# A two-layer hybrid backbone on one core: first output tile issued around the last attention unit's close, key copies ordered for the maxima, output tile steps with raised priority, wider lags

## The chip, the cores and the metric

The kernel runs on one core of one Trainium2 chip. The metric is device microseconds (us) from start to end of one execution. A core has TensorE (PE in the rows; PEld is its weight load), VectorE (DVE), ScalarE (ACT), GpSimd (POOL) and SyncE (SP). In this kernel SP issues nearly all transfers, in its program's order.

## The reference

Two layers work on 1024 latent tokens and 256 context tokens of 1024 features. Shortened to what matters:

```python
for l in range(DEPTH):                                    # DEPTH = 2
    mod_x = silu(c) @ w_ada[l] + b_ada[l]                 # shift, scale, gate
    hx, hc = modulate(x, ...), modulate(ctx, ...)         # RMS norm, scale, shift
    u_x, u_c = hx @ w_in[l], hc @ w_in[l]                 # one projection, cut into the branches
    a_x = rmsnorm(gdn_bidir(q, k, v, g, beta)) * silu(z)  # gated delta rule, chunks of 64, two directions
    b_x = softmax_attention(q_x, cat(k_x, k_c), cat(v_x, v_c)) * silu(z_b)    # 4 heads
    c_x = b_gate * dwconv(c_gate * h) * silu(z_c)
    x = x + gate_x * (cat(a_x, b_x, c_x) @ w_out[l])
    ...                                                   # the same for ctx in layer 0
return rmsnorm(x, final_norm_g)
```

The delta rule needs, for each 128 tokens, direction and head, the inverse of a triangular matrix.

## The kernel before

The tokens are ten tiles of 128 (tiles 8 and 9 are the context), in three groups: 512, 512 and 256 tokens. Matmuls that need float32 precision are three: operands are split into a high and a low part (`split`, L75 on ACT for the high part, L76 on DVE or POOL for the low one), and `mm3` (L84) and the blocks (L452) add hi·hi, lo·hi and hi·lo.

The order of the program is written by a planner. Pieces of work are generators ("lanes"), each `yield x` of which asks to be resumed when x us of planned matmul work have gone by; between them the main line emits block matmuls and calls `sch.tick`. What comes out is one program order. A scheduler then orders each engine's instructions by priority, with `tc.high_priority` to raise some. TensorE keeps the written order from the delta recurrence on (`in_order`) until the last attention unit's close. Tiles live in small pools that are used round: "P2" has 7 buffers for the raw weight slices `wr`, the gates `zb`, `ot` and `za` of the output tiles, the rows `mk` and `mq` of the attention projections and others, so that a load there waits for the reader of the buffer's previous tile.

In a layer these stages matter here:

- The **modulation** lane (`Ada`): 512 KB slices `wa` are loaded (L184), and the next resumption multiplies them (L188). In layer 0 the last of these run beside the projection.
- The **projection**: `run_blocks` multiplies weight blocks with all groups (L452), 24 matmuls for 512 tokens and 24 of half width for 256. Beside it the triangular inverses are made: `base_inverse` (L680, L681, DVE) and `merge`, one lane for each of the ten tiles, which joins 32-blocks to 64 and 128: four small matmul steps (L720, L729/L732, L746, L755) with copies on ACT and DVE between them, and a store of the result `nn_d` (L760).
- **Keys and values**: `kv_lane`, one for each tile, waits until merges are done, loads `mk` (L824), transposes it (L827, L828) and copies it (ACT, L79) to `ckv` and `pes`. From `pes` the position rows go by DMA into the key tensors `kh`, `kl` and `kc` (L1058, high, low and context). `q_rows` (L854, L855) does the like for queries.
- **Attention** in units of a token group and two heads. `a_max` (L1102, L1104) takes row maxima over the keys, `a_shift` (L1113, L1117) turns them and sends them into the queries, `a_scores` (L84, L1143) and `a_pv` (L1159) are the scores, exponentials and values; the exponentials are summed tile by tile on POOL (L1129), and the closing adds of the last key step of a unit's first head, and of both heads in the last unit, on DVE (L1127). `a_out` (L1166 to L1176) closes a unit: sums by matmul (L1170), reciprocal, gate. The first unit's maxima stand in a prologue with `k_pair` (keys of two heads) and `v_tile` (values of a tile).
- The **output**: `load_wo` brings the 16 slices of `w_out` (L1327) and splits them into two halves of 512 columns, `wo[0]` and `wo[1]`. `finish(i)`, one for each output tile, loads `ot`, `raw` and `za`, scales `ot` by its root mean square (squares L1344 on ACT, L1345 to L1349 on DVE and POOL), transposes it (L1353), multiplies by the gate (L1354), splits the result into `mix`, and multiplies it with both halves: 24 matmuls of 512 columns each (L84).

Of the kernel before, what the change touches and what calls it, by code (L numbers as in the profile page):

```python
# [18 lines left out]
EPS = 1e-6  # L19
# [9 lines left out]
def kernel(  # L29
# [27 lines left out]
    def st(shape, tag, dtype=F32, name=None):  # L57
        return sb.tile(shape, dtype, tag=tag, name=name or tag, bufs=BUFS[tag])
# [19 lines left out]
    def copy_a(out, in_):  # L78
        A.activation(out=out, in_=in_, func=ACTF.Copy)  # L79
# [97 lines left out]
    class Ada:  # L177
# [42 lines left out]
        def lane(self):  # L220
            todo = [(t, q, k4) for t in self.thirds for q in range(4) for k4 in range(2)]

            def get(n):
                wa = st([128, 4, 256], "P4", name="wa")
                self.load(*todo[n], wa)
                return wa

            for n, (t, q, k4) in enumerate(todo):
                if k4 == 0:
                    brow = self.bias(q) if t == 2 else None  # L230
                    pm = bank()
                wa = get(n)
                yield 6.5
                self.mm(k4, wa, pm)
                if k4 == 1:
                    yield 1.5
                    yield from self.close(t, q, pm, brow)
# [78 lines left out]
    for l in range(DEPTH):  # L316
# [372 lines left out]
        def merge(i, bt, tl):  # L689
            while not based.ok(bt):  # L690
                yield 1.0
            M = st([128, 4, 128], "P2", name="Mm")
            S.dma_start(out=M, in_=mm_d[i])
# [13 lines left out]
            with tc.high_priority(offset=400):  # L707
# [3 lines left out]
                for bk in range(4):  # L711
                    r = slice(32 * bk, 32 * bk + 32)
                    co = 32 * (bk % 2)
                    copy_a(nt6[r, :, co:co + 32], ntr[r, bk // 2])
            yield
            prs = ((0, 0, 1), (1, 1, 0), (0, 2, 3), (1, 3, 2))
# [5 lines left out]
            with tc.high_priority(offset=400):  # L722
                A.activation(out=Z, in_=z3, func=ACTF.Copy, scale=-1.0)
            yield
            n3 = bank()[:, 0:128].rearrange("p (h c) -> p h c", h=4)
# [8 lines left out]
            with tc.high_priority(offset=400):  # L734
# [4 lines left out]
                for q, (d, a, e) in enumerate(prs):  # L739
                    copy_a(N[32 * a:32 * a + 32, d, :, 32 * e:32 * e + 32], n3[32 * a:32 * a + 32])  # L740
            yield
            z23 = bank()[:, 0:256].rearrange("p (h c) -> p h c", h=4)
# [97 lines left out]
        def q_rows(g):  # L840
# [7 lines left out]
            if g < 2:  # L848
                rot = st([128, 512], "P2", name="rot")
                S.dma_start(out=rot[64:128], in_=rot_in[:, t0:t0 + n])  # L850
            yield 3.0
            pt0, pt1 = bank(), bank()
# [208 lines left out]
        def k_pair(h0):  # L1061
            ws = wk[:, :, 64 * h0:64 * h0 + 128]
            for g in (0, 1, 2):
                t0, n = GROUPS[g]
                cs = slice(t0, t0 + n)
                pk = bank()
                mm3(pk[:, 0:n], ((ws[:, 0], ckv[0][:, cs]), (ws[:, 0], ckv[1][:, cs]), (ws[:, 1], ckv[0][:, cs])))
                for r in range(2):
                    h = h0 + r
                    hi, lo = (kh[:, h, cs], kl[:, h, cs]) if g < 2 else (kc[:, 0, h, :], kc[:, 1, h, :])  # L1070
                    pr = pk[64 * r:64 * r + 64, 0:n]
                    copy_a(hi[0:64], pr)
                    if r:
                        kr = st([128, 512], "P2", name="kr")[0:64, 0:n]
                        copy_a(kr, pr)
                        P.tensor_tensor(lo[0:64], kr, hi[0:64].bitcast(F32), ALU.subtract)
                    else:
                        V.tensor_tensor(out=lo[0:64], in0=pr, in1=hi[0:64].bitcast(F32), op=ALU.subtract)
                yield


# [37 lines left out]
        def a_sums(u, kts, pts, rs=(0, 1)):  # L1119
            n = GROUPS[u["g"]][1]  # L1120
            keys = a_keys(u["g"])
            for r in rs:
                acc = vt[:, 5 + r, 0:n]
                ab_ = [pts[r][:, kk, 0:n] for kk in range(2)]
                for a0, a1 in [(ab_[0], ab_[1])] if kts[0] == keys[0] else [(acc, ab_[0]), (acc, ab_[1])]:
                    if kts[-1] == keys[-1] and (r == 0 or u is units[-1]):
                        V.tensor_tensor(out=acc, in0=a0, in1=a1, op=ALU.add)  # L1127
                    else:
                        P.tensor_tensor(acc, a0, a1, ALU.add)  # L1129
# [168 lines left out]
        v_tile(7)  # L1298
        a_shift(units[0])
        v_tile(8)  # L1300
        v_tile(9)
        for _ in k2:
            pass
        sch.tick(1.0)
        nu = len(units)
# [18 lines left out]
        def load_wo_half(q, wh, wl):  # L1324
            for k in range(KD):
                wr = st([128, 512], "P2", name="wr")
                S.dma_start(out=wr, in_=w_out[l, 128 * k:128 * k + 128, 512 * q:512 * q + 512])  # L1327
                yield 1.5
                split(wr, wh[:, k], wl[:, k], P if k % 2 else V)
                yield 1.5  # L1330

        def finish(i):
# [9 lines left out]
            jk = st([128, 128], "h5", name="jk4")  # L1342
            for h in range(4):
                A.activation(out=jk, in_=ot[:, h], func=ACTF.Square, accum_out=so[:, h:h + 1])  # L1344
            V.scalar_tensor_tensor(out=so, in0=so, scalar=1.0 / 128, in1=s_2[:, :, i], op0=ALU.mult, op1=ALU.mult)  # L1345
            P.tensor_scalar(so, so, 1.0, EPS, ALU.mult, ALU.add)
            P.tensor_tensor(so, so, nhalf[:, 0:4], ALU.pow)
            V.tensor_tensor(out=so, in0=so, in1=s_1[:, :, i], op=ALU.mult)
            V.tensor_tensor(out=ot, in0=ot, in1=bc(so, 128), op=ALU.mult)  # L1349
# [4 lines left out]
            V.scalar_tensor_tensor(out=raw[:, 0:4, :], in0=pt.rearrange("p (h f) -> p h f", h=4), scalar=col[:, 74:75], in1=za,  # L1354
                                   op0=ALU.mult, op1=ALU.mult)
            mix = st([128, 2, KD, 128], "W8", F32R, name="mix")
            split(raw[:, 0:4], mix[:, 0, 0:4], mix[:, 1, 0:4])
            split(raw[:, 4:8], mix[:, 0, 4:8], mix[:, 1, 4:8], P)
            xt = load_x(l, i)
            done[i] = xt  # L1360
            yield 3.5
            for q in range(2):
# [7 lines left out]
                if last:  # L1370
                    if q == 0:
                        sf = st([128, 2], "st", name="sf")
                    A.activation(out=tm, in_=xt[:, cs], func=ACTF.Square, scale=D ** -0.5, accum_out=sf[:, q:q + 1])
            if not last:
                S.dma_start(out=xs_d[i], in_=xt)
                return
# [29 lines left out]
        for x_, u in enumerate(units):  # L1406
# [12 lines left out]
            for q, kts in enumerate(steps):  # L1419
# [129 lines left out]
```

## Time and profile before

| | us |
|---|---|
| runs of the kernel | 1716.41, 1718.66, 1720.2 |
| their median | 1718.66 |
| the profiled execution, start to end | 1723.55 |
| its span, first to last instruction | 1721.8 |
| TensorE busy in the span | 1650.5 |

The granted clock is TensorE's share of full speed as the profile records it: 0.978 in the mean. Layer 0 takes about the first 950 us, layer 1 the rest. TensorE is busy nearly all the time, so that its idle stretches and what follows them are what to read; a table of waits gives, for each place, the total, how often, and the longest.

### The profile page before, as it was taken

What the parts mean: (1) busy time and instruction counts of PE and PEld (TensorE: products, weight loads), DVE (VectorE), ACT (ScalarE), POOL (GpSimd) and SP (SyncE); (2) the same over time, 40 slices, a digit from 0 to 9 for tenths busy, and PEclk for the clock granted to TensorE, in tenths of its full rate; (3) what the DMA queues carried; (4) which work ended last, traced back from release to release, by engine and by line L of the source; (5) the groups of instructions that cost most, each with busy time, mean ns of one, the idle gap of its engine ahead of it and who ended that gap; (6) DMA issues with size and microseconds to landing.
All of it is one profiled execution on the core that took longest, in us unless ns stands there. A gap on an engine that the chain in (4) does not pass through costs nothing.

```text
span 1721.8 us, 29896 instructions
## 1 busy us (share of the span) xinstructions
PE 1650.5 (96%) x10964; PEld 1316.9 (76%) x10964; DVE 1101.9 (64%) x2041; ACT 758.8 (44%) x1909; POOL 646.3 (38%) x848
## 2 busy tenths in 40 slices
PE   7999999999999999998999999999999989999998
PEld 5887888787887877764888887787778778776586
DVE  2534668878643767765565346689797377776664
ACT  4644565223444534344354435652245444434432
POOL 0520345321320456557331212544232136556731
PEclk8999999999999899999999999999999989999999
DMA  9332464753254755544443314556524465454551
GB/s 360 124 126 79 155 196 150 242 178 123 78 160 125 257 157 177 186 144 159 132 141 111 104 56 134 161 179 224 166 70 128 151 211 164 160 188 156 172 159 49
DMA packets 195403, 266.54 MB, mean 155 GB/s; under 512 B 50529, under 2 KB 115249, under 8 KB 195257
## 3 DMA queue, kind: packets, MB, share of 16 engines
q1 hardware_dynamic: 195256, 264.64, 47.8%
q8 instruction: 87, 1.43, 0.3%
q14 instruction: 60, 0.48, 0.1%
HBM read 182.71 MB, written 79.17 MB: 152 GB/s over the span
## 4 chain that ended last, share of the span: by engine, by line
PE 68%; DVE 10%; DMA 9%; issue 5%; ACT 3%; POOL 3%; SPq 1%; POOLq 0%; DVEq 0%; ACTq 0%
PE bank L452 26%; PE bank L84 22%; PE bank L1159 3%; PE bank L1236 2%; PE bank L1255 2%; PE bank L1249 2%; DVE pr L680 2%; PE bank L1254 2%; PE bank L1102 2%; DMA gcb<-row_d 2%; DVE Mb L681 1%; DMA wa<-in_w_ada_dram 1%; PE bank L1226 1%; DVE acc L466 1%; PE bank L516 1%
## 5 line engine op out<-in xcount | busy, mean ns | idle before, releaser
L452 PE MATMUL bank<-h_hi,w 128*128 128x512 f32 x1664 | 432.5, 403 | 2.4 <-DVE h_hi L283 2.4
L452 PEld LDWEIGHTS bank<-h_hi,w 128*128 128x128 f32 x1664 | 305.4, 190 | 74.6 <-issue 4.5
L452 PE MATMUL bank<-h_lo,w 128*128 128x512 f32 x832 | 217.7, 402 | 0.0
L452 PEld LDWEIGHTS bank<-h_lo,w 128*128 128x128 f32 x832 | 154.3, 189 | 37.0 <-issue 1.6
L466 DVE SCALAR_TENSOR_TENSOR acc<-pad,col,acc 128x1284 f32<-128x1284 f32 (+1 forms) x104 | 160.1, 1540 | 11.1 <-ACT acc L463 9.5
L1129 POOL TENSOR_TENSOR vt<-vt,probT 128x512 f32<-128x512 f32 x110 | 144.7, 1335 | 20.2 <-ACT probT L1143 19.5
L84 PE MATMUL bank<-wo_hi,mix 128*128 128x512 f32 x576 | 145.0, 402 | 1.8 <-ACT wo_hi L75 1.1
L1143 ACT ACTIVATE probT<-bank 128x512 f32<-128x512 f32 (+1 forms) x168 | 96.5, 590 | 98.2 <-PE bank L84 92.2
L84 PEld LDWEIGHTS bank<-wo_hi,mix 128*128 128x128 f32 x576 | 108.2, 191 | 28.6 <-ACT wo_hi L75 2.6
L76 DVE TENSOR_TENSOR w<-wr,w 128x1024 fp32r<-128x1024 f32 x52 | 66.6, 1283 | 93.3 <-ACT w L75 93.3
L1104 DVE TENSOR_REDUCE mx<-bank 128x1 f32<-128x512 f32 (+1 forms) x200 | 108.5, 585 | 10.9 <-PE bank L1102 9.7
L452 PE MATMUL bank<-h_c,w 128*128 128x256 f32 x816 | 109.7, 287 | 0.0
L452 PEld LDWEIGHTS bank<-h_c,w 128*128 128x128 f32 x816 | 102.2, 190 | 5.8 <-issue 3.7
L75 ACT ACTIVATE w<-wr 128x1024 fp32r<-128x1024 f32 x52 | 54.9, 1060 | 75.3 <-PE bank L452 56.3
L84 PE MATMUL bank<-qt,kh 97*128 97x512 f32 (+1 forms) x256 | 84.4, 411 | 3.5 <-ACT probT L1143 2.8
L1159 PE MATMUL bank<-probT,vt 128*64 128x512 f32 (+1 forms) x336 | 79.4, 594 | 0.0
L1232 POOL TENSOR_TENSOR ring<-ring,qx 128x512 f32<-128x512 f32 x32 | 40.9, 1277 | 92.7 <-DMA ring<-row_d 76.8
L680 DVE TENSOR_TENSOR pr<-L,Mb 128x31 f32<-128x31 f32 (+15 forms) x186 | 70.7, 380 | 4.6
L84 PE MATMUL bank<-wo_lo,mix 128*128 128x512 f32 x288 | 73.5, 395 | 0.0
L681 DVE TENSOR_TENSOR Mb<-Mb,pr 128x31 f32<-128x31 f32 (+15 forms) x186 | 68.6, 369 | 5.0
L617 POOL TENSOR_TENSOR gcb<-gcb,gc 128x1024 f32<-128x1024 f32 x20 | 44.5, 2231 | 62.7 <-DMA gcb<-row_d 36.8
L79 ACT ACTIVATE pad<-bank 128x512 f32<-128x512 f32 (+1 forms) x78 | 41.0, 531 | 54.1 <-PE bank L452 39.1
(310 smaller groups left out, 3225.2 us busy)
## 6 DMA issues: line engine op xcount, KB each, us to landing
wr<-in_w_blk_dram SPq DMA_DIRECT2D x52, 512.0 KB
wa<-in_w_ada_dram SPq DMA_DIRECT2D x32, 512.0 KB
gcb<-row_d SPq DMA_DIRECT2D x20, 512.0 KB
nn_d<-N SPq DMA_DIRECT2D x20, 512.0 KB
ring<-vr_d SPq DMA_DIRECT2D x40, 256.0 KB
ring<-nn_d SPq DMA_DIRECT2D x40, 256.0 KB
qk_d<-gcb SPq DMA_DIRECT2D x18, 512.0 KB
ring<-kt_d SPq DMA_DIRECT2D x36, 256.0 KB
```

Of the source, the lines that this page charges most:

```text
L75: A.activation(out=hi, in_=raw, func=ACTF.Copy)
L76: eng.tensor_tensor(out=lo, in0=raw, in1=hi.bitcast(F32), op=ALU.subtract)
L84: T.matmul(outp, lhsT=lh, rhs=rh, start=q == 0, stop=q == n - 1)
L452: T.matmul(pb[:, 0:n], lhsT=self.w[:, wi, k, :], rhs=hg[g][hi][:, k, :], start=q + k == 0, stop=q == 2 and k == KD - 1)
L466: V.scalar_tensor_tensor(out=acc[:, 2:hi], in0=pad[:, 2 + t - r:hi + t - r], scalar=col[:, ci:ci + 1], in1=acc[:, 2:hi], op0=ALU.mult, op1 ...
L617: P.tensor_tensor(gcb, gcb, bc(gc[:, i, :], 128), ALU.subtract)
L680: V.tensor_tensor(out=pv, in0=bc(L[:, 0:k, k], w), in1=N[:, k:k + 1, k:32].to_broadcast([128, k, w]), op=ALU.mult)
L681: V.tensor_tensor(out=N[:, 0:k, k:32], in0=N[:, 0:k, k:32], in1=pv, op=ALU.subtract)
L1104: V.tensor_reduce(mx[:, gk:gk + 1], pb[:, 0:n], AX.X, ALU.max)
L1129: P.tensor_tensor(acc, a0, a1, ALU.add)
L1143: A.activation(out=pts[r][:, kk, 0:n], in_=pb, func=ACTF.Exp)
L1159: T.matmul(u["po"][64 * r:64 * r + 64, 0:n], lhsT=vx[:, kt, hh * 64:hh * 64 + 64], rhs=pts[r][:, kk, 0:n], start=kt == keys[0], stop=kt == ...
```

## The change

Lags: a loaded `wa` slice is multiplied 8.5 instead of 6.5 planned us after its load; in `merge` three steps wait 4.5 instead of the default 3.0 until all three base inverses are done; `q_rows` waits 5.0 instead of 3.0 after its loads; the two steps of a `wo` slice wait 1.8 instead of 1.5. In the first `k_pair` only the first head's high key copies stand with the matmuls, and all the other copies come after the three groups. The first unit's shift comes after a value tile and the rest of the second `k_pair`. The closing adds of the last unit's second head go from DVE to POOL. In `finish` the scaling and the splits get raised priority, and a `yield` stands between the two halves. At the layer's end the sums of the last unit come after both halves of output tile 0.

```diff
@@ Ada.lane
-                yield 6.5
+                yield 8.5
                 self.mm(k4, wa, pm)
@@ merge
+            lag = 3.0 if len(based) == 3 else 4.5
...
-            yield
+            yield lag
             prs = ((0, 0, 1), (1, 1, 0), (0, 2, 3), (1, 3, 2))
...
@@ q_rows
-            yield 3.0
+            yield 5.0
@@ k_pair
+                    if r == 0:
+                        copy_a(hi[0:64], prs[0][0])
+                rest.append((n, prs))
+                if h0:
+                    k_rest(*rest.pop())
                 yield
+            for n, prs in rest:
+                k_rest(n, prs)
...
+        def k_rest(n, prs):
+            (p0, h0_, l0), (p1, h1, l1) = prs
+            kr = st([128, 512], "P2", name="kr")[0:64, 0:n]
+            copy_a(h1, p1)
+            copy_a(kr, p1)
+            V.tensor_tensor(out=l0, in0=p0, in1=h0_.bitcast(F32), op=ALU.subtract)
+            P.tensor_tensor(l1, kr, h1.bitcast(F32), ALU.subtract)
@@ a_sums
-                    if kts[-1] == keys[-1] and (r == 0 or u is units[-1]):
+                    if kts[-1] == keys[-1] and r == 0:
                         V.tensor_tensor(out=acc, in0=a0, in1=a1, op=ALU.add)
@@ prologue of attention
         v_tile(7)
-        a_shift(units[0])
         v_tile(8)
-        v_tile(9)
         for _ in k2:
             pass
+        a_shift(units[0])
+        v_tile(9)
@@ load_wo_half
-                yield 1.5
+                yield 1.8
                 split(wr, wh[:, k], wl[:, k], P if k % 2 else V)
@@ finish
+            with tc.high_priority(offset=400):
+                for h in range(4):
+                    A.activation(out=jk, in_=ot[:, h], func=ACTF.Square, accum_out=so[:, h:h + 1])
...
+            with tc.high_priority(offset=400):
+                V.scalar_tensor_tensor(out=raw[:, 0:4, :], in0=pt.rearrange("p (h f) -> p h f", h=4), scalar=col[:, 74:75], in1=za,
+                                       op0=ALU.mult, op1=ALU.mult)
...
+                if q == 0:
+                    yield
@@ end of the layer
-        a_pv(*prev)
         Q.clear()
         ahead(2)
-        sch.tick(2.0)
-        next(ending)
-        in_order.__exit__(None, None, None)
-        sch.tick(1.8)
+        a_pv(*prev)
+        sch.tick(3.0)
         sch.until(lambda: wof.ok(0))
         for q in range(3, n_act + 3):
+            if q == 3:
+                next(fg[0])
             ahead(q)
             next(fg[q - 3], None)
+            if q > 3:
+                next(fg[q - 3], None)
+            else:
+                next(ending)
+                in_order.__exit__(None, None, None)
```

Of the program's rows on TensorE where layer 1's projection ends and keys and values begin (N and tt are a merge's tiles, h_hi and h_lo the activations of a block), this stands in the kernel before:

```order
L452 MATMUL bank<-h_hi,w 128x512 x8
L452 MATMUL bank<-h_lo,w 128x512 x8
L452 MATMUL bank<-h_hi,w 128x512 x5
L755 MATMUL bank<-N,tt 64x64 x8
L452 MATMUL bank<-h_hi,w 128x512 x11
L827 MATMUL bank<-cst,mk 128x128
L828 MATMUL bank<-cst,mk 32x128
```

and after the change:

```order
L856 MATMUL bank<-cst,mq 64x128
L452 MATMUL bank<-h_lo,w 128x512 x8
L452 MATMUL bank<-h_hi,w 128x512 x8
L747 MATMUL bank<-tt,Mm 64x64 x8
L756 MATMUL bank<-N,tt 64x64 x16
L828 MATMUL bank<-cst,mk 128x128
L829 MATMUL bank<-cst,mk 32x128
```

Before, 40 more block matmuls stand between the pairs of the key transposes that follow; after, the last block matmul stands ahead of the last two merges' final steps, and the ten tiles' transposes follow one another without a break.

At the end of layer 1, TensorE's rows before (vt holds the sums of the exponentials, ot_15718, ot_15804 and ot_15875 are output tiles 0, 1 and 2):

```order
L1159 MATMUL bank<-probT,vt 64x512 x8
L1353 MATMUL bank<-cst,ot_15718 128x128 x4
L1170 MATMUL bank<-vt,cst 64x512
L1353 MATMUL bank<-cst,ot_15804 128x128 x4
L84 MATMUL bank<-wo_hi,mix 128x512 x7
L1170 MATMUL bank<-vt,cst 64x512
L84 MATMUL bank<-wo_hi,mix 128x512 x9
L84 MATMUL bank<-wo_lo,mix 128x512 x8
L84 MATMUL bank<-wo_hi,mix 128x512
L1353 MATMUL bank<-cst,ot_15875 128x128 x4
```

and after:

```order
L1170 MATMUL bank<-probT,vt 64x512 x4
L1365 MATMUL bank<-cst,ot_15718 128x128 x4
L1170 MATMUL bank<-probT,vt 64x512 x4
L84 MATMUL bank<-wo_hi,mix 128x512 x16
L84 MATMUL bank<-wo_lo,mix 128x512 x8
L1365 MATMUL bank<-cst,ot_15804 128x128 x4
L84 MATMUL bank<-wo_hi,mix 128x512 x16
L84 MATMUL bank<-wo_lo,mix 128x512 x8
L1181 MATMUL bank<-vt,cst 64x512 x2
```

The sums have moved from between the two transposes to behind both halves of tile 0; the second half, which was free to fall behind the other tiles' work, now stands ahead of it.

## Rows read from the trace of the kernel before

**Rows 1.** The page's first part: busy us, share of the span, instructions

```profile
PE 1650.5 (96%) x10964; PEld 1316.9 (76%) x10964; DVE 1101.9 (64%) x2041; ACT 758.8 (44%) x1909; POOL 646.3 (38%) x848
```

**Rows 2.** TensorE's waits: line, whom for, total us, times, longest us

```profile
PE bank L1102 <- DMA kc<-pes: 4.8, 2, 2.6
PE bank L1113 <- DVE nm L1107: 4.3, 2, 2.1
PE bank L1353 <- DVE ot L1349: 4.0, 3, 2.5
PE bank L746 <- DVE tt L738: 3.9, 2, 2.8
PE bank L729 <- ACT tt L723: 3.6, 2, 2.7
PE bank L720 <- issue: 3.5, 1, 3.5
PE bank L1170 <- DVE vt L1127: 3.1, 1, 3.1
...
PE bank L854 <- DMA mq<-mla_d: 1.1, 1, 1.1
```

**Rows 3.** Stretches of 10 us: busy us by engine, granted clock (PEclk), DMA share

```profile
310.00:320.00 10.00, 7.14 (x46) 6.13 (x45) 9.70 (x12) 0.00 (x0) 1.98 (x4) 0.84 0.93 282
...
580.00:590.00 10.00, 7.85 (x46) 6.99 (x46) 5.56 (x13) 6.64 (x20) 3.09 (x3) 0.83 0.38 132
...
820.00:830.00 10.00, 10.00 (x41) 7.98 (x40) 3.36 (x6) 1.93 (x9) 2.69 (x3) 0.90 0.31 91
1190.00:1200.00 10.00, 6.48 (x54) 5.30 (x53) 8.19 (x18) 3.53 (x8) 4.16 (x11) 0.71 0.56 172
...
1210.00:1220.00 10.00, 7.96 (x39) 6.67 (x39) 9.46 (x23) 1.53 (x3) 0.00 (x0) 0.66 0.39 116
1280.00:1290.00 10.00, 7.32 (x137) 6.23 (x136) 9.19 (x25) 5.37 (x17) 4.08 (x11) 0.83 0.18 49
...
1390.00:1400.00 10.00, 9.05 (x39) 8.11 (x40) 5.05 (x12) 0.97 (x2) 0.64 (x1) 0.55 1.01 375
1410.00:1420.00 10.00, 8.01 (x41) 7.13 (x42) 5.43 (x12) 4.35 (x12) 4.54 (x4) 0.83 0.32 100
```

**Rows 4.** TensorE's timeline: start us, us, engine, line, tiles [idle before, released by]

```profile
316.09 0.64 PE L188 MATMUL bank<-wa,csl 128*32 128x256 f32 x8 [2.86 <-DMA wa<-in_w_ada_dram]
```

**Rows 5.** ACT's timeline, a key tile's two copies in layer 1

```profile
1370.17 0.28 ACT L79 ACTIVATE ckv<-bank 128x128 fp32r<-128x128 f32 x1 [2.64 <-PE bank L828]
1370.46 0.26 ACT L79 ACTIVATE pes<-bank 32x128 fp32r<-32x128 f32 x1
```

**Rows 6.** SP's timeline, the issues into the context keys in layer 1

```profile
1381.75 4.06 SPq L1058 DMA_DIRECT2D kc<-pes  x4
```

**Rows 7.** End of layer 0: TensorE's first output matmuls, ACT's last `wo_hi` copy

```profile
807.11 4.58 PE L84 MATMUL bank<-wo_hi,mix 128*128 128x512 f32 x18 [0.67 <-ACT mix L75]
...
819.68 0.63 ACT L75 ACTIVATE wo_hi<-wr 128x512 fp32r<-128x512 f32 x1 [0.55 <-DMA wr<-in_w_out_dram]
```

**Rows 8.** End of layer 1: TensorE's sums and first output matmuls

```profile
1617.76 1.97 PE L1170 MATMUL bank<-vt,cst 128*64 128x512 f32 x2 [3.10 <-DVE vt L1127]
...
1620.42 2.03 PE L84 MATMUL bank<-wo_hi,mix 128*128 128x512 f32 x7
```

**Rows 9.** End of layer 1: ACT's first `mix` and last `wo_hi` copies, SP's last weight loads

```profile
1617.14 1.15 ACT L75 ACTIVATE mix<-raw 128x512 fp32r<-128x512 f32 x2 [6.02 <-DVE raw L1354]
...
1634.30 1.25 ACT L75 ACTIVATE wo_hi<-wr 128x512 fp32r<-128x512 f32 x2 [1.44 <-DMA wr<-in_w_out_dram]
...
1622.43 7.66 SPq L1327 DMA_DIRECT2D wr<-in_w_out_dram  x6
```

**Rows 10.** Adds of the exponentials by line: ns min/median/max, first and last start

```profile
L1127 DVE TENSOR_TENSOR vt<-vt,probT x18: 676/1327/1758, 638.7 to 1618.8; 128x512 f32<-128x512 f32 x18
...
L1129 POOL TENSOR_TENSOR vt<-vt,probT x110: 1257/1280/1743, 604.4 to 1614.6; 128x512 f32<-128x512 f32 x110
```

More of the change, by code (lines that the diff above doesn't have):

```diff
@@ L723, in merge @@
                 A.activation(out=Z, in_=z3, func=ACTF.Copy, scale=-1.0)
-            yield
+            yield lag
             n3 = bank()[:, 0:128].rearrange("p (h c) -> p h c", h=4)
@@ L740, in merge @@
                     copy_a(N[32 * a:32 * a + 32, d, :, 32 * e:32 * e + 32], n3[32 * a:32 * a + 32])
-            yield
+            yield lag
             z23 = bank()[:, 0:256].rearrange("p (h c) -> p h c", h=4)
@@ L1062, in k_pair @@
             ws = wk[:, :, 64 * h0:64 * h0 + 128]
+            rest = []
             for g in (0, 1, 2):
@@ L1067, in k_pair @@
                 mm3(pk[:, 0:n], ((ws[:, 0], ckv[0][:, cs]), (ws[:, 0], ckv[1][:, cs]), (ws[:, 1], ckv[0][:, cs])))
+                prs = []
                 for r in range(2):
@@ L1070, in k_pair @@
                     hi, lo = (kh[:, h, cs], kl[:, h, cs]) if g < 2 else (kc[:, 0, h, :], kc[:, 1, h, :])
[L1071 to L1078, printed above, removed]
-                yield
+                    prs.append((pk[64 * r:64 * r + 64, 0:n], hi[0:64], lo[0:64]))
+                    if r == 0:
[3 more added lines that the diff above has]
+                    k_rest(*rest.pop())
+                yield
+            for n, prs in rest:
[7 more added lines that the diff above has]
+            P.tensor_tensor(l1, kr, h1.bitcast(F32), ALU.subtract)
         def a_keys(g):
@@ L1327, in load_wo_half @@
                 S.dma_start(out=wr, in_=w_out[l, 128 * k:128 * k + 128, 512 * q:512 * q + 512])
-                yield 1.5
+                yield 1.8
                 split(wr, wh[:, k], wl[:, k], P if k % 2 else V)
-                yield 1.5
+                yield 1.8
         def finish(i):
@@ L1342, in finish @@
             jk = st([128, 128], "h5", name="jk4")
[L1343 to L1349, printed above, removed]
+            with tc.high_priority(offset=400):
+                for h in range(4):
+                    A.activation(out=jk, in_=ot[:, h], func=ACTF.Square, accum_out=so[:, h:h + 1])
+                V.scalar_tensor_tensor(out=so, in0=so, scalar=1.0 / 128, in1=s_2[:, :, i], op0=ALU.mult, op1=ALU.mult)
+                P.tensor_scalar(so, so, 1.0, EPS, ALU.mult, ALU.add)
+                P.tensor_tensor(so, so, nhalf[:, 0:4], ALU.pow)
+                V.tensor_tensor(out=so, in0=so, in1=s_1[:, :, i], op=ALU.mult)
+                V.tensor_tensor(out=ot, in0=ot, in1=bc(so, 128), op=ALU.mult)
             yield 3.0
@@ L1353, in finish @@
                 T.transpose(pt[:, h * 128:(h + 1) * 128], ot[:, h], ident)
-            V.scalar_tensor_tensor(out=raw[:, 0:4, :], in0=pt.rearrange("p (h f) -> p h f", h=4), scalar=col[:, 74:75], in1=za,
-                                   op0=ALU.mult, op1=ALU.mult)
             mix = st([128, 2, KD, 128], "W8", F32R, name="mix")
-            split(raw[:, 0:4], mix[:, 0, 0:4], mix[:, 1, 0:4])
-            split(raw[:, 4:8], mix[:, 0, 4:8], mix[:, 1, 4:8], P)
+            with tc.high_priority(offset=400):
+                V.scalar_tensor_tensor(out=raw[:, 0:4, :], in0=pt.rearrange("p (h f) -> p h f", h=4), scalar=col[:, 74:75], in1=za,
+                                       op0=ALU.mult, op1=ALU.mult)
+                split(raw[:, 0:4], mix[:, 0, 0:4], mix[:, 1, 0:4])
+                split(raw[:, 4:8], mix[:, 0, 4:8], mix[:, 1, 4:8], P)
             xt = load_x(l, i)
```

## Prediction

> **What bounds the kernel now.** I read the page's first part first: TensorE is busy 96% of the span, no other engine over 64% [rows 1]. So the span is TensorE's work, and a change that only moves work can take away TensorE's idle time, and what a slow clock costs, or add to them. Next comes the table of TensorE's waits [rows 2]: the reader is to see that the waits are few and single, each two or three microseconds long, and that they stand where one stage hands over to the next. Third are the stretches of 10 us around these waits [rows 3]: around and after a wait of two microseconds or more the granted clock shows 0.55 to 0.90, so in parts of such a stretch it is at 1.2 GHz, not 2.4. What that costs I take as (1 - granted clock) x 10 us for a stretch, an upper bound, since a part of it falls on idle time. So a wait of 2.5 us costs about 4 us.
>
> Since every tick of TensorE counts, each term below is idle time gone or come, with its clock. The sum is made against the profiled execution's 1723.55 us; the median of the runs shown is 1718.66, a factor of 0.9972.
>
> **The change part by part.**
>
> *Modulation lag.* One slice beside layer 0's projection is waited for 2.86 us [rows 4], and the stretch around it has a clock of 0.84, 1.6 us [rows 3]. In the new order its load, which follows the slice before, has one step of 8 block matmuls of 512 columns more between it and its use. A block or output matmul of that width takes 4.58 / 18 = 0.25 us [rows 7], so 2 us more cover the load and 0.9 stay, too short for the clock to fall after it. Bounds -4.5 and 0; I take **-3.5**.
>
> *Merges.* The three waits at the merge steps are 3.5 + 3.9 + 3.6 = 11.0 us [rows 2], the clock 2.9 + 3.4 + 1.7 = 8.0 us in three stretches [rows 3]; all of it is -19. The waits end with DVE or ACT (the one called "issue" stands at the first merge step, whose operand DVE has just turned and scaled). The longer lag gives each step 1.5 us more TensorE work in front. That helps where DVE was merely late, but DVE is busy 8.2 and 9.5 of 10 us there [rows 3], and a step moved back also has more DVE work queued ahead of it. I expect the wait at ACT's tt and the small ones to go with their clock and the two in the crowded stretch to be halved. Bounds -19 and 0; I take **-10**.
>
> *Queries' lag.* The wait at the mq load, 1.1 us [rows 2], goes: **-1**. Bounds -1 and 0.
>
> *The first shift.* It is waited for twice, 4.3 us in all [rows 2], with a clock of 0.83 after each, 3.4 us [rows 3]: -7.7 at best. The matmuls that now stand ahead of it (a value tile and the rest of the keys) take some 1.3 us of each wait of 2.1, by the pace of half-width matmuls, about half of 0.25 us. That leaves waits under a microsecond. Nothing else waits for the shift before the first scores, and the DMA of the shifted rows has the queries' matmuls in front of it. Bounds -7.7 and 0; **-4**.
>
> *Key copies and the bunch of key tiles.* Only the two first high copies now stand ahead of the maxima on ACT; the maxima that wait do so for the context keys, 4.8 us in two waits [rows 2], whose DMA is issued last of eight in layer 1 [rows 6]. It is now third of eight in layer 1 and second in layer 0, so that this wait should go. But the wider merge lag pushes the last merges behind the last block matmul in layer 1, and the ten key tiles behind them. A tile's two copies take 0.28 + 0.26 = 0.54 us of ACT [rows 5], ten of them 5.4; TensorE's transposes take less than half, and the block matmuls that covered the rest stand in front. So the keys' DMAs are issued some 5 to 6 us later against TensorE's work than before, with a wait for a merge's last step of a microsecond before it. In layer 1 that is +6.5, less 2.6 for the wait that goes: **+4**; bounds -3 and +8. The clock there is 0.55 already [rows 3], so I add none. In layer 0 block matmuls still stand among the first three tiles; the loss and the gain cancel: **0**, bounds -3 and +4.
>
> *Sums on POOL.* Four adds go from DVE to POOL. Row against row they take 1280 ns on POOL and 1327 on DVE in the median [rows 10]: nothing. The sums now stand behind both halves of tile 0, 48 matmuls or 11 us of cover; without it POOL's queue of these adds, 1.28 us each, would cost 3 to 5. The Trainium skill (GPSIMD Engine Reference, section 4, "When to use GPSIMD") speaks against the move: an elementwise add with two inputs is about twice as slow on GpSimd as on VectorE. The fastest add on DVE, 676 ns [rows 10], agrees with that, the median does not; by the rule the four adds would end 2.4 us later, which the cover hides as well, so the sum is the same by either.
>
> *The layers' ends.* The waits for ot (4.0 us, layer 0) and for the sums (3.1, layer 1) [rows 2] lose their cause: scaling is raised, and the sums have moved. The clock of 0.90 after layer 0's [rows 3] goes too: -5 and -3.1. But the second half of tile 0 now stands in TensorE's written order in front of the sums and of all later tiles, and it needs all eight slices of `wo[1]`. The six last loads of these take 7.66 us to issue in layer 1, and the last high copy starts at 1634.30 and takes 1.25 us for two [rows 9], so it ends at 1635.5. In the new order five stand in that place, one load or 1.3 us less: 1634.3. TensorE reaches the second half much sooner: tile 0's mix is there at about 1617.5 [rows 9], 24 matmuls take 5.6 us at the unhindered pace, so it stands from 1623 on, and goes through the high products as the slices come. Before, TensorE worked from 1620.42 on other tiles [rows 8]. By 1634 it had done some 13 us of output matmuls and 3 us of sums; the new order has 5.6 done, and some 1.6 of the slices at hand. It is 9 us behind less 1.6: **+7**. Bounds: -3.1 (slices in time) and +10.2, or +14.7 with a new low clock as after the longest stall here, 0.55 or 4.5 us [rows 3]. In layer 0 the first output matmuls start at 807.11 and the last copy ends at 820.3 [rows 7]: 24 matmuls, a transpose, and then some 7 us of waiting where before 4.0 stood; **+2.5**, bounds -5 and +5.7.
>
> *Slower weight lag, the yield in finish.* 0.3 planned us a step, 16 slices, issued while the attention still runs: hidden, unless a slice is already late, which the last term holds.
>
> Sum: -3.5 - 10 - 1 - 4 + 4 + 0 + 7 + 2.5 = **-5**: 1718.55 for the profiled execution, **1714** for the median, 0.3% under 1718.66. A measurement of this kernel tells about 0.2%, 3.4 us, from no change.
>
> **The rivals.**
>
> *The second half of tile 0 waits in full (slower).* Place: the end of both layers. If the slices of `wo[1]` are split no earlier than before, and the clock falls in the wait, the terms are +14.7 and +5.7 in place of 9.5 together: the sum is +5.9, 1729.45, a median of **1725**. For it: the last loads wait on the round use of P2, which the change leaves alone. Against it: the loads stand a dozen rows earlier on SP in layer 1. It decides from about 8.4 us over my term on, when the last high copy of layer 1 ends after 1635 and TensorE idles over 11 us before it.
>
> *DVE keeps up at the merges (faster still).* Then all -19 come: the sum is -14, 1709.55, **1705**. For it: each step gets more than one step's extra work when the lags add up. Against it: DVE's 9.5 of 10.
>
> *The lag does nothing there (same).* If DVE's backlog moves with the steps, only 5 of the 10 come: the sum is 0, a median of **1719**.
>
> **How the numbers follow.** The forecast has a chance of 0.32, the rival with DVE keeping up 0.19, the one without effect 0.21, the slower one 0.28. Faster by over 0.2% (under 1715.2) is 0.51, within it 0.21, slower 0.28. The forecast's own range is 1709 to 1719. The range of 8 in 10 takes in the rival on either side, 1705 and 1725, with a little for the bounds of the key tiles (+4 beyond my term) and of the first shift: 1701 to 1727.
>
> **What would show it.** The waits for wa (2.86), kc, nm and mq should be gone or about 1 us, with clocks near 1.00 where 0.84 and 0.83 stood. In the merges' stretch of layer 1 some 3 us of waiting should be left. At the start of layer 1's attention the ten pairs of transposes should stand at ACT's pace without block matmuls, and a wait for kh or kc behind them. At the ends a wait of 5 to 11 us on a `wo_hi` copy should stand in front of tile 0's second half. The prediction is wrong if that wait is under 2 us (then the time is near 1705), or if a new wait stands behind the sums on POOL.

## The result and the profile after

The changed kernel takes 1748.03 us in the median of five runs (1745.55 to 1750.81), the kernel before 1718.66 beside it. The ratio is 1.0171, with an interval of [1.0152, 1.019]: 29 us slower, where 0.3% faster was forecast. The profiled execution of the changed kernel is the one of 1750.81 us, with a span of 1749.1. Line numbers after the change are a few higher than before: L747 is the merge step that was L746, L1113 the maxima, L1124 the shift, L1181 the sums.

The page's first part and TensorE's largest waits, in the form of [rows 1] and [rows 2] (the wait for modulation slices, at the head here, is 12.9 us in five before the change):

```profile
PE 1662.1 (95%) x10964; PEld 1321.4 (76%) x10964; DVE 1098.9 (63%) x2038; ACT 760.6 (43%) x1909; POOL 635.0 (36%) x851
```

```profile
PE bank L188 <- DMA wa<-in_w_ada_dram: 14.4, 5, 6.6
PE bank L84 <- ACT wo_hi L75: 11.3, 11, 1.8
PE bank L516 <- ACT acc L495: 8.8, 1, 8.8
PE bank L1113 <- ACT qt L79: 7.5, 3, 4.0
PE bank L747 <- DVE tt L739: 5.8, 3, 2.8
PE bank L828 <- DMA mk<-mla_d: 5.2, 3, 4.1
...
PE bank L1365 <- DVE so L1360: 2.6, 1, 2.6
```

TensorE's instructions are the same 10964, and the waits for kc and mq of [rows 2] are gone. Others are new or larger: for the high copies of the output weights, for a convolution's `acc` (a wait that the kernel before does not have), for the queries, for a merge's `tt` (one of 2.62 us in layer 0 is new), and for the key rows `mk`.

How much each stage took is read from TensorE's timeline, by the start of the first maxima, the first scores, the end of the last values (`a_pv`), the first block matmul of layer 1, and TensorE's end. Worked out from these starts in each trace, in us:

| stage | before | after | difference |
|---|---|---|---|
| layer 0 up to the first maxima | 557.1 | 565.1 | +8.0 |
| its attention prologue, to the first scores | 35.9 | 37.1 | +1.2 |
| its attention, to the end of values | 210.0 | 216.5 | +6.5 |
| its output, to layer 1's first block | 130.9 | 134.6 | +3.7 |
| layer 1 up to its first maxima | 449.3 | 461.5 | +12.2 |
| its attention prologue | 35.5 | 27.2 | -8.3 |
| its attention | 195.3 | 193.1 | -2.2 |
| its output, to TensorE's end | 100.2 | 106.3 | +6.1 |

A wait that moves from the prologue to the place ahead of the first maxima changes both rows, so the two are best taken together: up to the first scores layer 0 takes 9.2 us more, layer 1 3.9.

The stretches of 10 us of the changed kernel around the new waits (columns as in [rows 3]), at the queries of layer 0, the weight slices, and before and at the convolution:

```profile
565.00:575.00 10.00, 7.21 (x27) 5.82 (x28) 5.52 (x12) 3.50 (x10) 5.67 (x5) 0.54 0.95 295
...
830.00:840.00 10.00, 6.83 (x14) 4.05 (x15) 4.85 (x5) 4.12 (x10) 4.00 (x3) 0.60 0.58 163
1250.00:1260.00 10.00, 10.00 (x90) 7.86 (x89) 3.53 (x5) 0.70 (x3) 1.99 (x5) 1.00 0.47 119
...
1300.00:1310.00 10.00, 3.32 (x13) 3.12 (x14) 9.82 (x9) 3.20 (x5) 3.11 (x5) 0.51 0.34 82
```

and one of the kernel before:

```profile
1240.00:1250.00 10.00, 10.00 (x69) 7.69 (x68) 3.61 (x4) 2.57 (x5) 3.11 (x5) 1.00 0.69 200
```

From 1300 on DVE is busy 9.8 of 10 us and TensorE 3.3, at a clock of 0.51. That DVE has little to do some 50 us earlier (3.5 of 10 us) is not the change's work: the kernel before has such a stretch too, 3.6 from 1240 on, some 300 us into the layer as here. What is new is how late the convolution gets its `acc`. In the changed kernel (TensorE, ACT and DVE):

```profile
1275.05 0.36 ACT L79 ACTIVATE pad<-bank 128x256 f32<-128x256 f32 x1
...
1294.47 0.68 PE L756 MATMUL bank<-N,tt 64*64 64x64 f32 x16
1295.33 1.38 ACT L463 ACTIVATE acc<-pad,col 128x1284 f32<-128x1284 f32 x1 [3.42 <-DVE pr L680]
1298.92 7.86 DVE L466 SCALAR_TENSOR_TENSOR acc<-pad,col,acc 128x1284 f32<-128x1284 f32 x5
```

```profile
1306.68 2.39 PE L516 MATMUL bank<-cst,acc 128*128 128x128 f32 x10 [8.85 <-ACT acc L495]
...
1402.84 0.45 PE L828 MATMUL bank<-cst,mk 128*128 128x128 f32 x1 [4.07 <-DMA mk<-mla_d]
...
1414.94 0.50 PE L1113 MATMUL bank<-kh,qt 96*128 96x512 f32 x1 [3.38 <-ACT qt L79]
```

and in the kernel before:

```profile
1260.61 0.36 ACT L79 ACTIVATE pad<-bank 128x256 f32<-128x256 f32 x1
...
1268.37 0.68 PE L755 MATMUL bank<-N,tt 64*64 64x64 f32 x16
1269.22 1.37 ACT L463 ACTIVATE acc<-pad,col 128x1284 f32<-128x1284 f32 x1 [3.55 <-issue]
```

`acc`, the convolution's `pad`, a merge's `tt` and the base inverse's two tiles all come from one pool of five buffers, "T5". In both kernels ACT's first pass over `acc` starts 0.2 us behind the last matmuls of the layer's third merge, which read that merge's `tt`: `acc` waits until a merge gives its buffer back. (The row of the changed kernel names a DVE instruction that ended in the same moment; with the merge lag alone, below, the row names the merge.) Before the change it starts 8 us after the last copy into its `pad`, after the change 20. Its taps on DVE (L466) then stand behind the rest of a base inverse, and TensorE waits 8.85 us for them.

At the end of layer 0, TensorE's second half of output tile 0 takes the slices one at a time:

```profile
826.37 0.48 PE L84 MATMUL bank<-wo_hi,mix 128*128 128x512 f32 x1
828.64 0.49 PE L84 MATMUL bank<-wo_hi,mix 128*128 128x512 f32 x1 [1.79 <-ACT wo_hi L75]
829.90 0.49 PE L84 MATMUL bank<-wo_hi,mix 128*128 128x512 f32 x1 [0.77 <-ACT wo_hi L75]
831.65 1.43 PE L84 MATMUL bank<-wo_hi,mix 128*128 128x512 f32 x2 [1.26 <-ACT wo_hi L75]
834.16 1.44 PE L84 MATMUL bank<-wo_hi,mix 128*128 128x512 f32 x2 [1.08 <-ACT wo_hi L75]
836.30 4.21 PE L84 MATMUL bank<-wo_hi,mix 128*128 128x512 f32 x9 [0.70 <-ACT wo_hi L75]
```

That is 5.6 us of waiting in pieces. On SP the last six loads of the weights take 6.66 us to issue from 826.64 on, one after the other.

### The profile page after: what moved, and what is told of

It reads as the page before. It is cut to its first block, busy times and chain, and to the rows that moved or that the text cites. A ratio compares the mean times of both kernels' runs of the same rounds, so it can differ in the third digit from the quotient of the medians.

```text
span 1749.1 us, 29902 instructions
## 1 busy us (share of the span) xinstructions
PE 1662.1 (95%) x10964; PEld 1321.4 (76%) x10964; DVE 1098.9 (63%) x2038; ACT 760.6 (43%) x1909; POOL 635.0 (36%) x851
## 5 line engine op out<-in xcount | busy, mean ns | idle before, releaser
L466 DVE SCALAR_TENSOR_TENSOR acc<-pad,col,acc 128x1284 f32<-128x1284 f32 (+1 forms) x104 | 163.2, 1570 | 9.0 <-ACT acc L463 7.1
L84 PE MATMUL bank<-wo_hi,mix 128*128 128x512 f32 x576 | 152.9, 415 | 12.5 <-ACT wo_hi L75 11.3
L84 PEld LDWEIGHTS bank<-wo_lo,mix 128*128 128x128 f32 x288 | 55.5, 193 | 13.6
```

The source lines that it names most:

```text
L84: T.matmul(outp, lhsT=lh, rhs=rh, start=q == 0, stop=q == n - 1)
L466: V.scalar_tensor_tensor(out=acc[:, 2:hi], in0=pad[:, 2 + t - r:hi + t - r], scalar=col[:, ci:ci + 1], in1=acc[:, 2:hi], op0=ALU.mult, op1 ...
```

## The experiments

Ratios are to the kernel before on the same chip, with 95% intervals. First the changed kernel with one part put back at a time.

**The layer's end put back**

```diff
-        Q.clear()
-        ahead(2)
         a_pv(*prev)
-        sch.tick(3.0)
+        Q.clear()
+        ahead(2)
+        sch.tick(2.0)
+        next(ending)
+        in_order.__exit__(None, None, None)
+        sch.tick(1.8)
         sch.until(lambda: wof.ok(0))
...
```

> The changed kernel with the layer's end put back: the last unit's values and sums, and both halves of an output tile issued together, as before. Theory A (written order): the second half of output tile 0 stands in front of everything else and waits for the last slices of the output weights; of the 29 us lost, some 13 to 16 come from the two ends, so 1731 to 1736 us, and the waits of output matmuls for the high copies of the weights (11.3 us in the changed kernel) fall to 1 or 2. Rival: the ends only take up what is late upstream, so putting them back gives 1744 to 1750.

Measured: 1739.32 us, ratio 1.0089 [1.0055, 1.0123]. The waits for high copies are gone from the list of those over half a microsecond. The two output stages take 130.8 and 102.3 us instead of 134.6 and 106.3, layer 0's attention 213.9 instead of 216.5. Theory A holds for the waits, and the time lies above its range and below the rival's. By the ratios the end costs 0.8% or 14 us (some 0.4 to 1.2%, if the two intervals are taken together); the two profiled executions differ by 8.8 us in their spans, and the rest lies within the runs' spread. Upstream, all is as late as in the changed kernel, the convolution's wait too (8.99 us).

**The merge lag put back**

```diff
-            lag = 3.0 if len(based) == 3 else 4.5
...
-            yield lag
+            yield
...
```

> The changed kernel with the merge lag put back to 3.0. Theory B (held buffers): the longer lag keeps the merges' tiles in their round-used pools, so that a convolution, the modulation slices and the key rows come late; 10 to 14 us of the loss are its own, so 1734 to 1738, without the 8.85 us wait of a convolution's transposes and with block matmuls between the key transposes again. Rival, that the lag helps at the merges and the loss is elsewhere: 1750 to 1757, with the merge steps' waits of about 10 us back.

Measured: 1731.35 us, ratio 1.006 [1.0039, 1.0081]: 1.1% or 19 us of the loss are the lag's, more than theory B's 10 to 14. The wait for `acc` is gone. So is that for `mk`, layer 1 takes 448.5 us up to its first maxima instead of 461.5, and layer 0 554.1 instead of 565.1. Two of the merges' waits of layer 1 stand as before the change:

```profile
1212.48 1.34 PE L746 MATMUL bank<-tt,Mm 64*64 64x64 f32 x16 [2.91 <-DVE tt L738]
...
1285.74 0.23 PE L729 MATMUL bank<-tt 32*32 32x32 f32 x4 [3.10 <-ACT tt L723]
```

Together they are 6 us. In the changed kernel one such wait of 2.81 us is left in layer 1, at 1263.86; so the lag had taken some 3 us away there, and brought several times that in their place. (In layer 0 it brought one: 2.62 us at 384.79.)

**The key copies put back**

```diff
-                    if r == 0:
-                        copy_a(hi[0:64], prs[0][0])
+                    copy_a(hi[0:64], pr)
+                    if r:
+                        kr = st([128, 512], "P2", name="kr")[0:64, 0:n]
...
```

> The changed kernel with the key copies in their old order. Theory C (ACT's queue): the copies that were put together after the three key groups stand ahead of the rotated queries on ACT, so the first maxima wait longer (7.5 us for the queries now, 2.6 before); then 1741 to 1745, with that wait at 2 to 4 us and some of the waits for the context keys back. Rival, that the key tiles' bunching alone makes the maxima late: 1746 to 1750, no difference.

Measured: 1750.12 us, ratio 1.0157 [1.0129, 1.0185], not told apart from the changed kernel. Theory C fails, and its rival's time came: the queries are still waited for 6.7 us, not 2 to 4, in two pieces a layer (3.09 and 1.05 us in layer 0, 1.25 and 1.34 in layer 1) where the changed kernel has one of 3.96 and one of 3.38, and no wait for the context keys is back.

**All lags put back**

```diff
-                yield 8.5
+                yield 6.5
...
-            yield 5.0
+            yield 3.0
...
-                yield 1.8
+                yield 1.5
```

and the merge lag as above.

> The changed kernel with all lags put back: modulation 6.5, merge 3.0, queries 3.0, output weights 1.5. By theory B with the merge lag alone at fault the same time as with only that put back, within 3 us; if the lag of the modulation slices (its wait grew from 2.9 to 3.9 us) or that of the output weights costs too, 3 to 8 us less, 1727 to 1733. If the lags help and the ends and key copies hold the whole loss, 1750 or more.

Measured: 1729.37 us, ratio 1.0047 [1.0028, 1.0066], not told apart from the merge lag alone put back. Of the lags, that of the merges does the harm.

Next, what about the longer lag and about the new end is it that costs.

**The lag in front of a merge, not inside it**

```diff
             while not based.ok(bt):
                 yield 1.0
+            if len(based) < 3:
+                yield 4.5
             M = st([128, 4, 128], "P2", name="Mm")
```

with the steps at the default 3.0.

> The changed kernel with the merges' extra 4.5 planned us put in front of a merge, before it takes any tile, instead of between its steps: a merge ends as late as in the changed kernel, but holds its tiles as short as before. Theory B (held buffers): the projection of layer 1 takes 448 to 452 us again, as with the old lag, not 461, and DVE does not run dry there; 1736 to 1742 us, some of the loss staying since the key tiles still come late. Rival (lateness): what costs is that merges end late; then the projection stays at 458 or more and the time at 1745 to 1752.

Measured: 1740.39 us, ratio 1.0108 [1.0076, 1.014]. The wait for `acc` is gone, and layer 1 takes 455.4 us up to its maxima, about midway between 461.5 and 448.5; layer 0 takes 559.7, midway between 565.1 and 554.1. What stays is this:

```profile
1264.80 0.68 PE L757 MATMUL bank<-N,tt 64*64 64x64 f32 x16 [3.13 <-ACT tt L751]
...
1390.53 0.33 PE L829 MATMUL bank<-cst,mk 128*128 128x128 f32 x1 [3.04 <-DMA mk<-mla_d]
1392.33 0.45 PE L829 MATMUL bank<-cst,mk 128*128 128x128 f32 x1 [1.08 <-DMA mk<-mla_d]
```

So both theories have a part. The tiles are held no longer than with the old lag, the convolution's wait is gone, and 0.6% of the 1.1% with it. The other 0.5% stays although nothing is held longer: the merges still end late, and the key rows are loaded behind them. About half each is a rough split, and not only for the intervals: the last merge's last step starts 439 us into layer 1, against 443 in the changed kernel and 425 with the old lag, and 539 us into layer 0, against 548 and 526, so that a part of the lateness went too. Whether other pools (P2, P4) are starved beside T5 was not tried.

**Nothing to wait for in tile 0's second half**

```diff
-                wh, wl = wo[q]
+                wh, wl = wo[0 if i == act[0] else q]
```

> The changed kernel in which the second half of output tile 0 multiplies with the first half of the output weights (the wrong half: the same matmuls in the same order, but nothing to wait for). Theory A (the slices come late): the waits of output matmuls for high copies fall from 11.3 us to under 3, the two ends get 3 to 6 us shorter each, the ratio to the kernel before falls from 1.017 to 1.010 to 1.013. Rival: the order of sums and halves itself costs (the next tiles are not ready either, the wait only moves on to tile 1): 1.015 to 1.019.

The product of tile 0 with the second half of the weights is left out in this kernel.

Measured: 1739.91 us, ratio 1.0096 [1.0058, 1.0133]. Layer 0's output takes 123.6 us, 11 less than in the changed kernel. With the attention ahead of it, which the new end makes longer, it is 340.0 us, against 351.1 in the changed kernel and 340.9 before: by these profiled executions the late slices are the whole loss of that layer's end. In layer 1 nothing is won (108.6 us against 106.3). TensorE has no wait in the second half of tile 0 there, but a long one at the next transpose:

```profile
1651.18 1.12 PE L1365 MATMUL bank<-cst,ot 128*128 128x128 f32 x4 [9.63 <-DVE ot L1361]
```

```profile
1634.97 5.92 SPq L1338 DMA_DIRECT2D wr<-in_w_out_dram  x5
1642.67 0.33 SPq L1347 DMA_DIRECT2D ot<-o_d  x1
```

SP issues the next tile's `ot` behind the five last weight slices. There theory A and its rival meet: the wait moves on to the next thing that SP brings.

**Weight slices with a lag of 1.2**

```diff
-                yield 1.8
+                yield 1.2
```

> The changed kernel with the lag of an output weight slice at 1.2 instead of 1.8, everything else as changed: in the written order 13 of 16 slices are then loaded ahead of the last output inputs in layer 0 (10 in the changed kernel), 12 in layer 1. Theory A (the slices come late for the second half of tile 0): the waits for high copies fall from 11.3 us to 2 to 6, ratio 1.010 to 1.014. Rival (buffers set when the slices can be loaded, not the lag): waits at 9 us or more, ratio 1.016 or more.

Measured: 1750.68 us, ratio 1.0185 [1.0164, 1.0206], no gain. The waits for high copies over half a microsecond fall to some 6 us, and layer 0's output stage to 127.8 us, so the lag does set when the slices come. But the output stage of layer 1 stays at 106.9 us and its attention grows to 197.7 from 193.1, where splits now run among it. Neither theory had that.

The two parts that lose, each alone on the kernel before:

**The new end alone** (the diff of the change's last part and the `yield` between halves)

```diff
+            if q == 3:
+                next(fg[0])
             ahead(q)
             next(fg[q - 3], None)
+            if q > 3:
+                next(fg[q - 3], None)
+            else:
+                next(ending)
+                in_order.__exit__(None, None, None)
```

> The kernel before with the new layer's end alone (sums behind both halves of tile 0, the yield between halves). If its loss is its own, and not one that other parts of the change bring, 1.005 to 1.009; rival, that with the old weight lag of 1.5 and without raised priority the slices are in time: 0.998 to 1.003.

Measured: 1733.51 us, ratio 1.0079 [1.0062, 1.0097]. The loss is its own: its two output stages take 134.9 and 106.4 us, as in the changed kernel, and layer 0's attention 215.1, so that attention and output are 9.1 us longer in layer 0 and 5.2 in layer 1 than before. There are single waits of up to 2.86 us for high copies, at the old lag of 1.5.

**The merge lag alone**

```diff
+            lag = 3.0 if len(based) == 3 else 4.5
...
-            yield
+            yield lag
```

> The kernel before with the merge lag of 4.5 alone. If the lag does the harm by itself, 1.009 to 1.014, with a convolution's transposes waiting 7 us or more in layer 1 and key transposes in one block; rival, that it needs the other lags to do harm: 0.998 to 1.005.

Measured: 1737.53 us, ratio 1.0102 [1.0086, 1.0118]. The convolution's wait is there without any other edit, and here the profile names a merge's last step as what `acc` waits for, 20 us after the last copy into `pad`:

```profile
1264.04 0.37 ACT L79 ACTIVATE pad<-bank 128x256 f32<-128x256 f32 x1
...
1284.60 1.37 ACT L463 ACTIVATE acc<-pad,col 128x1284 f32<-128x1284 f32 x1 [3.42 <-PE bank L756]
...
1296.26 2.40 PE L516 MATMUL bank<-cst,acc 128*128 128x128 f32 x10 [9.15 <-ACT acc L495]
```

0.79% and 1.02% make 1.81%; the whole change has 1.71%, which the intervals do not tell from it. What the remaining parts are worth the last three runs measure.

**End and merge lag put back, the rest kept** (the first two diffs together)

> The changed kernel with both the layer's end and the merge lag put back; what stays is the modulation, query and output weight lags, the key copies, the shift, the sums on POOL and the raised priority. If the two losses add up (0.8% and 1.1% by the earlier runs) the ratio to the kernel before is 0.998, 0.995 to 1.000: the rest is worth 2 to 8 us. Rival: the two share a cause, so that putting both back gives no more than 1.004.

Measured: 1716.23 us, ratio 0.9966 [0.9951, 0.9982], 0.34% faster than the kernel before. The two losses add up, and the rest together is a gain. The first maxima start at 555.96 instead of 557.15, and the prologues take 32.9 and 31.5 us instead of 35.9 and 35.5.

**End and all lags put back** (what stays are the key copies, the shift, the sums on POOL and the raised priority)

> The kernel before with the key copies, the shift, the sums on POOL and the raised priority alone (the layer's end and all lags put back). By the stages of the earlier runs the key copies and the shift win some 2 us in each prologue, and the sums on POOL make the last unit's close 1 to 2 us later: ratio 0.997 to 1.001. If the lags of modulation and queries are what helped, it is 0.2% or more above the kernel that keeps these; if they hurt, below it.

Measured: 1718.1 us, ratio 0.998 [0.9958, 1.0001], not told apart from the version above or from the kernel before.

**End, merge lag and sums put back**

```diff
-                    if kts[-1] == keys[-1] and r == 0:
+                    if kts[-1] == keys[-1] and (r == 0 or u is units[-1]):
```

on the version with end and merge lag put back.

> The changed kernel with the layer's end, the merge lag and the sums (back on DVE) put back. With end and merge lag alone put back the ratio was 0.9966, and TensorE waited 5.2 us for the sums at the end of layer 1 where the kernel before waits 3.1. If the adds on POOL cause the longer wait, it falls to about 3 us and the ratio to 0.994 to 0.996. Rival: raised priority of the output tiles on DVE delays the sums; then the wait stays at 4.5 or more and the ratio at 0.996 to 0.998.

Measured: 1715.32 us, ratio 0.9969 [0.9957, 0.9981]. The end of layer 1 with the adds on POOL, and then with the adds on DVE:

```profile
1610.98 1.97 PE L1180 MATMUL bank<-vt,cst 128*64 128x512 f32 x2 [5.18 <-DVE vt L1137]
```

```profile
1606.32 1.97 PE L1180 MATMUL bank<-vt,cst 128*64 128x512 f32 x2 [3.31 <-DVE vt L1137]
```

The wait falls as expected, by 1.9 us, but the time does not move beyond its interval. The wait does not end with an add on POOL, though. It ends with the closing add of the first head, which stays on DVE in both kernels (L1137). What stands ahead of that add on DVE is the scaling of an output tile; with the adds on POOL, and then on DVE:

```profile
1599.70 7.88 DVE L1360 TENSOR_TENSOR ot<-ot,so 128x512 f32<-128x512 f32 x1
1607.50 1.75 DVE L1137 TENSOR_TENSOR vt<-vt,probT 128x512 f32<-128x512 f32 x1
```

```profile
1596.68 1.74 DVE L1360 TENSOR_TENSOR ot<-ot,so 128x512 f32<-128x512 f32 x1
1603.27 1.73 DVE L1137 TENSOR_TENSOR vt<-vt,probT 128x512 f32<-128x512 f32 x1 [4.85 <-POOL vt L1139]
```

The same instruction takes 7.88 us beside nine adds in a row on POOL, and 1.74 beside seven. By their ratios these two versions, with end and merge lag put back and with the sums as well, are the fastest of the study, and the only ones faster than the kernel before beyond their intervals.

## Why the prediction was wrong, point by point

**The merges: the step that failed.** It stood as a gain between -19 and 0, -10 taken, since "the longer lag gives each step 1.5 us more TensorE work in front". The lag cost 1.0 to 1.1%, 17 to 19 us. For the waits that it named the argument held: layer 1 has 9.0 us of them before the change (3.5, 2.8 and 2.7) and 3.2 after, as the prediction's "some 3 us" had it. What failed is the bound of 0: the steps' lag was counted as cover alone. One price of it the prediction did see, in the term of the key copies: the merges end later and the key tiles bunch, +6.5 in layer 1, where TensorE now waits 4.9 us for key rows (4.07 and 0.82). The other price stood at nothing: a merge with longer steps holds its tiles longer in a pool that others use too, so that the convolution's `acc` comes late, with a wait of 8.85 us and a clock of 0.51 around it. The experiment with the lag in front of the merge gives holding and lateness about half each. No case of the forecast and no rival held a loss at the merges, and the range ended 21 us short. The trace of before had a warning that the rows chosen do not show: the convolution's `acc` already started right behind a merge's last step (1269.22 after 1268.37 + 0.68).

**The layers' ends: right in kind, too small in layer 0.** +2.5 and +7 stood in the sum, and the slower rival had 20.4 together. (The figures given for +7 make 13 + 3 - 5.6 - 1.6 = 8.8; the 1.6 was taken off twice.) By the ratios the end costs 0.8%, 14 us (put back, or alone on the kernel before); by the stages of the kernel with the new end alone, 9.1 in layer 0 and 5.2 in layer 1: the loss lies mostly where the smaller term stood. The wait in layer 0 is 5.6 us in pieces against some 7 foreseen, since the slices are taken as they come; what was missed is the clock of 0.60 behind it, and that a transpose of tile 0, with a wait of 2.6 us for its scaling, now stands ahead of the last values. That the wait is for the slices was shown by the kernel in which tile 0's second half needs none: layer 0 then gains 11 us. That layer 1 gains nothing there was not foreseen: the loads of the next tile's inputs stand behind those of the weights on SP.

**Key copies.** +4 for layer 1 and 0 for layer 0 stood in the sum. The waits for kc [rows 2] went, and a block of ten key tiles with a wait behind it came as said, but as a part of the merge lag's loss. In the changed kernel the copies make no difference that can be measured (1.0157 with the old order, against 1.0171), and the waits for kc are gone with the old order too. With the end and all lags put back, where the copies stay, the wait for kc is replaced by one for the rotated queries: 3.37 us in layer 0 and 3.36 in layer 1, where the kernel before has 1.29 + 2.24 and 1.30 + 2.59. ACT copies these queries behind the second head's keys. In the timeline of ACT in the changed kernel that copy is last:

```profile
562.47 1.20 ACT L79 ACTIVATE kh<-bank 64x512 fp32r<-64x512 f32 x2
563.68 0.77 ACT L79 ACTIVATE kc<-bank 64x256 fp32r<-64x256 f32 x2
564.48 0.62 ACT L79 ACTIVATE qt<-r 32x512 fp32r<-32x512 f32 x1
```

The prediction read the copies as leaving ACT's queue to the maxima; it did not look at what the queries had in front of them there, and so counted 2.6 us as won of which some 0.5 were.

**The small terms.** The shift was to win 4 us. It is still waited for, 1.86 and 1.87 us against 2.1 and 2.1 [rows 2]: half a microsecond. In layer 0 the trace now puts the wait down to a copy on ACT, in layer 1 still to DVE's maxima; the matmuls moved ahead of the shift did not cover it. The modulation slice was to win 3.5: in the changed kernel its wait grew from 2.86 [rows 4] to 3.87 us, with the merge lag put back it fell to 1.17, with a second one of 1.72 behind it. The wait for mq [rows 2] went, 1 us, but not by the queries' lag: it is gone with all lags put back too.

**Sums on POOL.** They were costed at nothing under the cover of tile 0, and in the changed kernel no wait for them stands. Without the cover they cost 1.9 us of waiting, not the 3 to 5 of POOL's queue that were foreseen, and by a way that was not foreseen: the slow scaling on DVE beside them. The Trainium skill (GPSIMD Engine Reference, section 4, "When to use GPSIMD") has a two-input add about twice as slow on GpSimd as on VectorE. In this place the traces do not show that: the four closing adds on DVE take 4.76 us together (1.73, 1.28 for two, 1.75), and nine adds on POOL 12.01 us, 1.33 each, so that four would take 5.3.

**What stays open.** Whether other pools than T5 starve under the merge lag; where the 11 us go that layer 0 loses by it up to its first maxima, since no new wait there is as long as the convolution's; why a scaling on DVE takes 7.88 us beside adds on POOL, for which no run was made; and why the remaining parts together win 0.34%, of which key copies and shift show as 3 to 4 us shorter prologues, but none of them was run alone on the kernel before.

## What to carry to other kernels

A longer lag between the steps of a piece of work is not only cover: its tiles are held longer in pools that others wait for, and its end moves too, so both belong in the sum as losses before the wait that it hides is counted as a gain. Wait in front of the first tile, not between steps, if the pool is shared. Before a piece of work is put into a written order ahead of all else, look up when its last input lands and what else the engine could have done until then; and bound an edit of a schedule from both sides, unless something in the profile excludes the loss.

## What the runs showed of the hardware

The forecast took waits under a microsecond or so as too short for the clock to fall. In the changed kernel five waits of 0.70 to 1.79 us, from 826.9 to 836.3 with a matmul or two between them, came with a granted clock of 0.60 in the stretch from 830 to 840, nearly as low as the 0.51 of the stretch from 1300 to 1310, which holds most of the single wait of 8.85 us. In parts of that stretch TensorE was at 1.2 GHz, not 2.4, while it was busy 6.83 of its 10 us: the nine matmuls from 836.30 on take 4.21 us, 0.47 each, against the 0.25 of [rows 7]. For a single short wait the forecast's reading holds: in the kernel before, behind the 1.07 us at 600.28, the clock is 1.00 from 600 to 610.

Where adds stood in a row on POOL, a two-input instruction of DVE could take several times as long: the scaling of an output tile, 128x512, took 7.88 us beside nine such adds, with the end and merge lag put back. It took 7.89 us with the end alone put back and 7.93 with the end and all lags put back, beside nine adds each time. Its median in the same kernel is 0.69 us, and its longest in the kernel before, beside seven adds, 1.75.
